# Sharing out the expert gathers of a two-layer encoder: 8 : 8 : 7 over three chunks, and 110 instead of 50 left for the next layer

## The chip, the cores and the metric

The kernel runs on one core of a Trainium2 chip. The metric is the time of one execution on the device in microseconds (us). A run is timed several times; the figure of a kernel is the median.

## What is computed

The reference runs two layers over 512 tokens of width 1024, one sequence. Each layer is an attention stage and an expert stage:

```python
for l in range(DEPTH):                                    # 2
    sh1, sc1, g1, sh2, sc2, g2 = split(silu(c) @ ada_w[l] + ada_b[l], 6)
    h = modulate(x, sh1, sc1)                             # layer norm, scale, shift
    mix = hybrid_mixer(h, ...)                            # three kinds of heads, one w_in, one w_o
    x = layer_norm(ALPHA * x + (1 + g1) * mix, ln1_g[l], ln1_b[l])
    h = modulate(x, sh2, sc2)
    # peer: per token and head, the 16 best of 128 * 128 experts
    q = (h @ wq).reshape(S, 8, 2, 128)
    v1, i1 = top_k(q[..., 0, :] . sub_k1, 16); v2, i2 = top_k(q[..., 1, :] . sub_k2, 16)
    experts, g = best 16 of the 16 * 16 sums v1 + v2, softmax of them
    act = gelu(u_tab[experts] . h)                        # u_tab, v_tab: 16384 rows of 1024 f32
    ffn = sum over the 8 * 16 experts of (g * act) * v_tab[experts]
    x = layer_norm(ALPHA * x + (1 + g2) * ffn, ln2_g[l], ln2_b[l])
```

## The kernel before

The 512 tokens are four blocks of 128. The attention stage of a layer handles blocks 0 and 1 first and then 2 and 3: `prepare` normalises a block's rows of x (`xs0` to `xs3`; tile `ytok`, line 253), `project` multiplies by w_in (two blocks share each weight tile; its first vector step on a block is `kr`, L407), `attend` does the heads (`mx` L506, `sm` L513, `pr` L515), `output` multiplies by w_o, `between` does the two normalisations around the residual sum, `queries` multiplies by the query weights and takes the 16 best keys (`tk_v`, L617), and `topk` (L624) picks the experts: 16 pairs of `tk_hot` (VectorE, L665), `tk_pick` (GpSimd) and `tk_ef` (VectorE, L668), then `eidx` (L669).

The expert sums are done in two ways. Blocks 1 and 2 (`DENSE`) run through **all** experts: `dense` goes over 128 rows of 128 experts each. It loads the row's part of both tables (`u`, `v`, 512 KB each, issued by SyncE), transposes u on TensorE (`utp`, L817), splits it into a rounded half and the rest (`uh` ScalarE L819, `ul` VectorE L821), multiplies (`sp`, L831 to L833), applies the gelu and the gate tile G (`ge`, L837) and accumulates (`acc`, L849). G is built in three chunks of 43, 42 and 43 expert rows (`CUTS`): the first chunk before row 0, the second while the rows of the first are done, the third while those of the second are done (`build`: `o` on VectorE, `pg` on TensorE, L804). In the rows of the third chunk nothing is built.

Blocks 0 and 3 are **gathered**: `experts` fetches, for each of the 128 slots of a token, one row of `u` and one of `v` per partition with an indirect DMA from GpSimd's queue (512 KB, tile `g`, four buffers, L696 and L708), and VectorE reduces each in one instruction (a dot product L698, or a weighted sum L713). This text calls such an instruction a gather sum. A layer has 2 blocks x 2 tables x 128 = 512 of them. When all sums of a block are done, `finish` writes the block's new rows of x (`xs0`, `xs3`), which the next layer's `prepare` reads.

`experts` is a generator, and `pace(ex, mark, n)` takes n steps from it. The calls to `pace` share the 512 gathers of a layer out: `EARLY[l]` ahead of the dense part, one beside each of the 32 builds of the first chunk, `LATE[l]` at the start of the next layer's attention stage (L903), and the rest beside the 128 expert rows (L955). A scheduler then orders each engine's instructions; what is written earlier has the higher priority. Each engine takes its instructions strictly in that order.

Of the kernel before, what the change touches and what calls it, by code (L numbers as in the profile page):

```python
# [30 lines left out]
PH, NK, TOPK = 8, 128, 16  # L31
TG = 8
TI = 2
CUTS = (0, 43, 85, 128)
DENSE = (1, 2)
EARLY = (80, 110)
LATE = (50, 0)
WK = 4
ADK = 2
HB = 2  # L40
# [13 lines left out]
def body(ctx, tc, x, c, positions, ada_w, ada_b, w_in, q_norm_g, kv_norm_g, w_uq, w_ukv, conv_w,  # L54
# [16 lines left out]
    def open_attention(l):  # L71
        A.stack = ExitStack()
        A.fix = A.stack.enter_context(tc.tile_pool(name=f"afix{l}", bufs=1))
        A.w = A.stack.enter_context(tc.tile_pool(name=f"aw{l}", bufs=1))
        A.bufs = BUFS[l]
        A.work = A.stack.enter_context(tc.tile_pool(name=f"awork{l}", bufs=1))
        A.small = A.stack.enter_context(tc.tile_pool(name=f"asmall{l}", bufs=2))
        A.ps = A.stack.enter_context(tc.tile_pool(name=f"aps{l}", bufs=1, space=PSUM))
        if l == 0:
            A.ad = A.stack.enter_context(tc.tile_pool(name="ad", bufs=1))  # L80
# [208 lines left out]
    def layer_setup(l):  # L289
        y = Layer()  # L290
        y.l = l
        y.hT = {}
        y.sc1 = A.fix.tile([P, KT], F32, name="sc1")
        nc.sync.dma_start(y.sc1, mod[l, D:2 * D].rearrange("(k p) -> p k", p=P))
        y.sh1 = A.fix.tile([P, KT], F32, name="sh1")
        nc.sync.dma_start(y.sh1, mod[l, 0:D].rearrange("(k p) -> p k", p=P))
        y.qg = A.fix.tile([P, 2], F32, name="qg")
        nc.sync.dma_start(y.qg, q_norm_g[l].rearrange("(k p) -> p k", p=P))
        y.kvg = A.fix.tile([P, 1], F32, name="kvg")
        nc.sync.dma_start(y.kvg, kv_norm_g[l].rearrange("(k p) -> p k", p=P))  # L300
        y.cw = A.fix.tile([P, 2, 3], F32, name="cw")
        for ci in range(2):
            nc.sync.dma_start(y.cw[:, ci, :], conv_w[l, :, ci * P:(ci + 1) * P].rearrange("w p -> p w"))
        y.sqT = A.fix.tile([P, 2, HS, P], F32, name="sqT")
        nc.vector.memset(y.sqT, 0.0)
        y.kT = A.fix.tile([QH + NB, HM, S], F32, name="kT")
        maskk = block_rows(64, P, NEG)
        nc.scalar.copy(y.kT[QH:QH + NB].rearrange("p h (b k) -> p h b k", b=NB),
                              maskk[QH:QH + NB, None, :, :].to_broadcast([NB, HM, NB, P]))
        y.v = A.fix.tile([P, NB, HM * VD], F32, name="v")  # L310
        y.skT = A.fix.tile([P, 2, S], F32, name="skT")
        y.sv = A.fix.tile([P, NB, HS * DS], F32, name="sv")
        y.uT = A.fix.tile([P, 2, P + 2], F32, name="uT")
        nc.vector.memset(y.uT[:, :, 0:2], 0.0)
        return y

    def layer_rows(y):
        l = y.l
        y.rows = rows[l]
        rf = A.work.tile([96, 256], F32, name="rf", tag="q", bufs=2)  # L320
        r = 0
        for src in (ln1_g[l:l + 1, :], ln1_b[l:l + 1, :], mod[l:l + 1, 4 * D:5 * D], mod[l:l + 1, 3 * D:4 * D],
                    mod[l:l + 1, 5 * D:6 * D], ln2_g[l:l + 1, :], ln2_b[l:l + 1, :],
                    mod[l:l + 1, 2 * D:3 * D]):
            nc.sync.dma_start(rf[r:r + 4, :], src.rearrange("o (c n) -> (o c) n", n=256))
            r += 4
        for p in range(3):
            if p:
                nc.sync.dma_start(rf[32 * p:32 * p + r, :], rf[0:r, :])
            q = slice(32 * p, 32 * p + 32)  # L330
            for k in range(p + 1):
                nc.vector.tensor_copy(rows[l][q], rf[q])
                if k < p:
                    nc.vector.tensor_tensor(rf[q], rf[q], rows[l][q], op=OP.subtract)

    def layer_keys(y):
        l = y.l
        y.keysT = A.fix.tile([P, 2 * PH, NK], F32, name="keysT")
        for i, src in enumerate((peer_k1, peer_k2)):
            kst = A.w.tile([P, PH, P], F32, name="kst", tag="w", bufs=A.bufs["w"])  # L340
            nc.sync.dma_start(kst, src[l].rearrange("h n d -> n h d"))
            for h0 in range(0, PH, 4):
                pt = A.ps.tile([P, 4, P], F32, name="pt", tag="tr", bufs=2)
                for j in range(4):
                    nc.tensor.transpose(pt[:, j, :], kst[:, h0 + j, :], ident)
                nc.scalar.copy(y.keysT[:, 2 * h0 + i:2 * (h0 + 4) + i - 1:2, :], pt)
# [11 lines left out]
    def prepare(y, b):  # L358
        hT = A.work.tile([P, KT, P], F32, name="hT", bufs=2)
        yt = A.work.tile([P, D], F32, name="ytok", bufs=1)  # L360
        normalize(yt, xs[b])
        transpose_cols(hT, yt, KT, scale=y.sc1, bias=y.sh1)
        y.hT[b] = hT
# [210 lines left out]
    def between(y, b, rt, mk=None):  # L574
        l = y.l
        row_op(y, rt, rt, 7, OP.mult, mk)
        nc.vector.scalar_tensor_tensor(rt, xs[b], ALPHA, rt, op0=OP.mult, op1=OP.add)
        affine(y, xs[b], rt, rt, 0, 1, mk)
        h2 = A.work.tile([P, D], F32, name="h2d", tag="tok", bufs=2)
        affine(y, h2, h2, xs[b], 2, 3, mk)  # L580
        h2T = A.work.tile([P, KT, P], F32, name="h2T", tag="tok", bufs=2)
        transpose_cols(h2T, h2, KT, tag="tr" if mk else "mm")
        if b in DENSE:
            slot = DENSE.index(b) * P
            nc.sync.dma_start(h2scr[l][:, :, slot:slot + P], h2T)
        else:
            nc.sync.dma_start(h2tok[l][b // 2], h2)
        v1 = topp.tile([P, 2 * PH, TOPK], F32, name="tk_v", bufs=2)
        fi = topp.tile([P, PH, 2, TOPK], F32, name="tk_f", bufs=2)
        return h2T, v1, fi  # L590
# [303 lines left out]
    def pace(ex, mark, n):  # L894
        gate[0] = mark
        for _ in range(n):
            next(ex)

    ada_first(range(4))
    for l in range(L):  # L900
        if l:
            open_attention(l)
            late()  # L903
        y = layer_setup(l)

        def pick(b, v1, fi):
            return topk(l, v1, fi, b, b not in DENSE)

        res = [None] * NB
        for b in (0, 1):  # L910
            prepare(y, b)
        layer_keys(y)
        ps = project(y, (0, 1))
        if l + 1 < L:
            ada_side(0, range(4, 12))
        layer_rows(y)
        behind = None
        for p in ps:
            b = p[0]
            attend(y, *p)  # L920
            if b == 1:
                for b2 in (2, 3):
                    prepare(y, b2)
            h = between(y, b, output(y, b, p[2]))
            r = queries(y, *h, range(4))
            if b == 0:
                behind = r
            res[b] = pick(b, *h[1:])
        p2, p3 = project(y, (2, 3), behind)
        if l + 1 < L:  # L930
            ada_side(1, range(12))
        attend(y, *p2)
        h = between(y, 2, output(y, 2, p2[2]))
        queries(y, *h, range(2))
        attend(y, *p3)
        rt = output(y, 3, p3[2])
        queries(y, *h, range(2, 4))
        res[2] = pick(2, *h[1:])
        h = between(y, 3, rt, lambda: A.ps.tile([P, 512], F32, name="prow", tag="at", bufs=2))
        queries(y, *h, range(4))  # L940
        res[3] = partial(pick, 3, *h[1:])
        A.stack.close()
        dn = dense(y, DENSE, res)
        ex = chain.from_iterable(experts(y, b, *res[b]) for b in range(NB) if b not in DENSE)
        pace(ex, None, EARLY[l])
        groups = 2 * P // TG
        for _ in range(groups):
            mark = next(dn)
            pace(ex, mark, 1)
        with tc.issue_after(mark.ins):  # L950
            res[3] = res[3]()
        n = 2 * 2 * NSLOT - EARLY[l] - LATE[l] - groups
        for a, mark in enumerate(dn):
            if a < NK:
                pace(ex, mark, (a + 1) * n // NK - a * n // NK)  # L955
        late = partial(pace, ex, mark, LATE[l])
        if not l + 1 < L:
            late()
# [22 lines left out]
```

## Time and profile before

| | us |
|---|---|
| median of three runs | 3564.16 |
| lowest, highest | 3544.61, 3568.53 |
| profiled execution, its span | 3550.53, 3548.8 |

The profile is one execution, so its stretches add up to its own span, some 14 us under the median. Over the whole span TensorE is busy 87%, VectorE 78%, GpSimd 42% and ScalarE 26%. [...]

### The profile page before, as it was taken

What the parts mean: (1) busy time and instruction counts of PE and PEld (TensorE: products, weight loads), DVE (VectorE), ACT (ScalarE), POOL (GpSimd) and SP (SyncE); (2) the same over time, 40 slices, a digit from 0 to 9 for tenths busy, and PEclk for the clock granted to TensorE, in tenths of its full rate; (3) what the DMA queues carried; (4) which work ended last, traced back from release to release, by engine and by line L of the source; (5) the groups of instructions that cost most, each with busy time, mean ns of one, the idle gap of its engine ahead of it and who ended that gap; (6) DMA issues with size and microseconds to landing.
All of it is one profiled execution on the core that took longest, in us unless ns stands there. A gap on an engine that the chain in (4) does not pass through costs nothing.

```text
span 3548.8 us, 54489 instructions
## 1 busy us (share of the span) xinstructions
PE 3072.0 (87%) x19708; PEld 2258.0 (64%) x19708; DVE 2765.7 (78%) x6277; ACT 927.4 (26%) x1860; POOL 1476.2 (42%) x1347
## 2 busy tenths in 40 slices
PE   7889768658999999999948896776699999999998
PEld 4657536536777776777736774555467767777775
DVE  4668996999777877776675579889998778776777
ACT  2342432222222222222222223312222222222221
POOL 1025573256343334444462045534454434444543
PEclk9989889859999999999979996997699999999998
DMA  9777978568898888899986586885789988989997
GB/s 276 221 230 251 313 261 287 174 187 282 306 322 307 316 310 310 311 348 344 337 288 206 173 292 211 296 294 178 238 275 350 333 312 316 331 323 335 358 353 256
DMA packets 430173, 1012.14 MB, mean 285 GB/s; under 512 B 40504, under 2 KB 229192, under 8 KB 429904
## 3 DMA queue, kind: packets, MB, share of 16 engines
q0 software_dynamic: 147456, 536.94, 42.5%
q1 hardware_dynamic: 282448, 471.73, 39.6%
q8 instruction: 156, 2.56, 0.3%
q14 instruction: 113, 0.93, 0.1%
HBM read 1002.06 MB, written 6.34 MB: 284 GB/s over the span
## 4 chain that ended last, share of the span: by engine, by line
PE 13%; DVE 13%; DMA 10%; issue 9%; POOL 4%; ACT 1%; SPq 0%; POOLq 0%; DVEq 0%; ACTq 0%
DMA g<-in_peer_v,eidx 5%; PE pm L157 4%; PE acc L849 3%; DVE acc L713 2%; POOL g L696 2%; DVE g L698 2%; DMA g<-in_peer_u,eidx 2%; DVE tk_ef L668 1%; PE sp L831 1%; PE sp L832 1%; PE sp L833 1%; PE utp L817 1%; DMA wt<-in_peer_wq 1%; POOL g L708 1%; DVE o L797 1%
## 5 line engine op out<-in xcount | busy, mean ns | idle before, releaser
L708 POOL DMA_INDIRECT g<-in_peer_v,eidx x512 | 613.4, 1198 | 782.0 <-DVE acc L713 481.7
L849 PE MATMUL acc<-v,ge 128*128 128x512 f32 x2048 | 928.9, 595 | 6.4 <-DVE ge L837 5.8
L696 POOL DMA_INDIRECT g<-in_peer_u,eidx x512 | 603.2, 1178 | 764.4 <-DVE g L698 499.9
L713 DVE SCALAR_TENSOR_TENSOR acc<-g,wts,acc 128x1024 f32<-128x1024 f32 x508 | 674.2, 1327 | 145.1 <-DMA g<-in_peer_v,eidx 137.7
L698 DVE SCALAR_TENSOR_TENSOR g<-g,h 128x1024 f32<-128x1024 f32 x512 | 620.3, 1225 | 172.9 <-DMA g<-in_peer_u,eidx 161.8
L831 PE MATMUL sp<-hh,uh 128*128 128x256 f32 x2048 | 613.7, 300 | 1.6 <-ACT ge L835 0.9
L849 PEld LDWEIGHTS acc<-v,ge 128*128 128x128 f32 x2048 | 370.3, 190 | 370.7 <-issue 364.1
L833 PE MATMUL sp<-hh,ul 128*128 128x256 f32 x2048 | 594.8, 290 | 0.0
L832 PE MATMUL sp<-hl,uh 128*128 128x256 f32 x2048 | 583.7, 285 | 0.0
L819 ACT CAST uh<-utp 128x512 fp32r<-128x512 f32 x512 | 304.1, 595 | 871.9 <-PE utp L817 710.9
L821 DVE TENSOR_TENSOR ul<-utp,uh 128x512 fp32r<-128x512 f32 x512 | 347.6, 684 | 110.5 <-ACT uh L819 104.2
L831 PEld LDWEIGHTS sp<-hh,uh 128*128 128x128 f32 x2048 | 392.4, 192 | 7.6 <-issue 5.5
L832 PEld LDWEIGHTS sp<-hl,uh 128*128 128x128 f32 x2048 | 392.1, 191 | 5.3 <-issue 5.3
L833 PEld LDWEIGHTS sp<-hh,ul 128*128 128x128 f32 x2048 | 391.4, 191 | 0.1
L817 PE MATMUL utp<-ident,u 128*128 128x128 f32 x2048 | 302.9, 277 | 49.0 <-DVE ul L821 46.5
L817 PEld LDWEIGHTS utp<-ident,u 128*128 128x128 f32 x2048 | 236.4, 142 | 126.9 <-issue 70.7
L806 ACT COPY G<-pg 128x344 f32<-128x344 f32 (+1 forms) x192 | 146.8, 765 | 593.9 <-PE pg L804 477.5
L804 PEld LDWEIGHTS <-o 128*128 128x128 bf16 x4608 | 163.3, 102 | 187.4 <-issue 91.9
L804 PE MATMUL pg<-o,o 128*128 128x43 bf16 (+1 forms) x4608 | 183.9, 190 | 104.7 <-DVE o L797 86.4
L157 PE MATMUL pm<-wt,h2T 128*128 128x256 f32 x1024 | 235.9, 385 | 17.6 <-DMA wt<-in_peer_wq 16.7
L157 PE MATMUL pm<-wt,hT 128*128 128x256 f32 (+1 forms) x1024 | 232.4, 380 | 12.6 <-ACT hT L274 6.3
L157 PEld LDWEIGHTS pm<-wt,h2T 128*128 128x128 f32 x1024 | 193.3, 193 | 51.0 <-DMA wt<-in_peer_wq 21.5
(235 smaller groups left out, 3448.2 us busy)
## 6 DMA issues: line engine op xcount, KB each, us to landing
u<-in_peer_u SPq DMA_DIRECT2D x256, 512.0 KB
v<-in_peer_v SPq DMA_DIRECT2D x256, 512.0 KB
wt<-in_peer_wq SPq DMA_DIRECT2D x128, 512.0 KB
adw<-in_ada_w SPq DMA_DIRECT2D x160, 256.0 KB
wt<-in_w_o SPq DMA_DIRECT2D x64, 512.0 KB
wt<-in_w_in SPq DMA_DIRECT2D x56, 512.0 KB
wt<-in_ada_w SPq DMA_DIRECT2D x16, 512.0 KB
g<-in_peer_u,eidx POOLq DMA_INDIRECT x512
```

What stands on the lines that cost most here:

```text
L157: r = nc.tensor.matmul(pm[:, c0:c0 + m], lhsT=lhsT[:, k0 + k, :], rhs=wt[:, k, :m], start=k0 + k == 0, stop=k0 + k == KT - 1)
L696: nc.gpsimd.indirect_dma_start(out=g, out_offset=None, in_=u_flat, in_offset=bass.IndirectOffsetOnAxis(ap=eidx[:, h, k:k + 1], axis=0))
L698: after(nc.vector.scalar_tensor_tensor(out=g, in0=g, scalar=1.0, in1=h2, op0=OP.mult, op1=OP.mult, accum_out=dots[:, h, k:k + 1]))
L708: nc.gpsimd.indirect_dma_start(out=g, out_offset=None, in_=v_flat, in_offset=bass.IndirectOffsetOnAxis(ap=eidx[:, h, k:k + 1], axis=0))
L713: r = nc.vector.scalar_tensor_tensor(out=acc, in0=g, scalar=wts[:, h, k:k + 1], in1=acc, op0=OP.mult, op1=OP.add)
L804: nc.tensor.matmul(pg[:, tt, 0:n], lhsT=o2[:, tt // TI, :, tt % TI], rhs=o1a[:, tt // TI, p, 0:n, tt % TI], start=tt == 0 and p == 0, stop ...
L817: nc.tensor.transpose(pt[:, j * P:(j + 1) * P], u[:, k * P:(k + 1) * P], ident)
L821: nc.vector.tensor_tensor(ul.rearrange("p j t -> p (j t)"), pt, uh.rearrange("p j t -> p (j t)").bitcast(F32), op=OP.subtract)
L831: nc.tensor.matmul(sp, lhsT=uh[:, j, :], rhs=hh[:, k, :], start=k == 0, stop=False)
L832: nc.tensor.matmul(sp, lhsT=uh[:, j, :], rhs=hl[:, k, :], start=False, stop=False)
L833: nc.tensor.matmul(sp, lhsT=ul[:, j, :], rhs=hh[:, k, :], start=False, stop=k == KT - 1)
L849: nc.tensor.matmul(acc[i][g], lhsT=w[:, i * P:(i + 1) * P], rhs=v[:, g * 512:(g + 1) * 512], start=a == 0, stop=a == NK - 1)
```

## The change

The number of gathers of layer 0 that wait for layer 1's attention stage goes from 50 to 110, and the gathers beside the expert rows are no longer spread evenly: a row of the chunks 0, 1 and 2 has the weight 8, 8 and 7. For layer 0 that leaves 512 - 80 - 110 - 32 = 290 beside the rows instead of 350. For layer 1 it stays at 370, with the new weights.

```diff
 EARLY = (80, 110)
-LATE = (50, 0)
+LATE = (110, 0)
+SHARE = (8, 8, 7)
...
         n = 2 * 2 * NSLOT - EARLY[l] - LATE[l] - groups
+        upto = [0]
+        for s, (c0, c1) in zip(SHARE, zip(CUTS, CUTS[1:])):
+            upto += [upto[c0] + s * (i + 1) for i in range(c1 - c0)]
         for a, mark in enumerate(dn):
             if a < NK:
-                pace(ex, mark, (a + 1) * n // NK - a * n // NK)
+                pace(ex, mark, upto[a + 1] * n // upto[NK] - upto[a] * n // upto[NK])
         late = partial(pace, ex, mark, LATE[l])
```

In the changed program the lines behind L37 are one further on, so that the gather sums are L699 and L714 there. What the scheduler makes of it on VectorE, at three places. The first is the start of the heads of block 0 in layer 1, before; 53 gather sums of layer 0 stand ahead of it, and none are left:

```order
L244 BN_STATS bnst<-acc 128x6 x2
L506 TENSOR_REDUCE mx<-sc 128x4
L246 BN_AGGR bnmv<-bnst 128x2
L232 SCALAR_TENSOR_TENSOR acc<-acc,bnmv,prow 128x512
L506 TENSOR_REDUCE mx<-sc 128x4
L232 SCALAR_TENSOR_TENSOR acc<-acc,bnmv,prow 128x512
L513 RECIPROCAL sm<-sm 128x4
L515 TENSOR_TENSOR pr<-pr,sm 128x512
L232 SCALAR_TENSOR_TENSOR xs_98<-acc,rs_r,prow 128x512 x2
```

The same place after (`xs_98` is `xs3`):

```order
L507 TENSOR_REDUCE mx<-sc 128x4
L699 SCALAR_TENSOR_TENSOR g,dots<-g,h_11911 128x1024
L507 TENSOR_REDUCE mx<-sc 128x4
L699 SCALAR_TENSOR_TENSOR g,dots<-g,h_11911 128x1024
L514 RECIPROCAL sm<-sm 128x4
L516 TENSOR_TENSOR pr<-pr,sm 128x512
L699 SCALAR_TENSOR_TENSOR g,dots<-g,h_11911 128x1024 x3
L514 RECIPROCAL sm<-sm 128x4
L516 TENSOR_TENSOR pr<-pr,sm 128x512
```

Again 53 gather sums stand ahead, and from there to `eidx` of block 0 another 60 stand between the attention's own steps. The finish of block 3 has gone from here. Second, where it now stands: among the last steps of `topk` of block 0, after.

```order
L233 SCALAR_TENSOR_TENSOR xs_98<-acc,rs_r,prow 128x512
L666 TENSOR_TENSOR tk_hot<-iotaj,tk_tib 128x400
L669 TENSOR_REDUCE tk_ef<-tk_pick 128x8
L247 BN_AGGR bnmv<-bnst 128x2 x2
L233 SCALAR_TENSOR_TENSOR rt<-rt,bnmv,prow 128x512 x2
L254 TENSOR_SCALAR ytok<-xs_98,bnmv,rs_r 128x1024
L233 SCALAR_TENSOR_TENSOR xs_96<-rt,rs_r,prow 128x512 x2
L670 CAST eidx_17995<-tk_ef 128x128
```

Before, that `ytok` of block 3 stood ahead of the first `tk_v` of block 0, one `ytok` behind the other:

```order
L253 TENSOR_SCALAR ytok<-xs_97,bnmv,rs_r 128x1024
L232 SCALAR_TENSOR_TENSOR h2d<-h2d,rs_r,prow 128x512 x2
L246 BN_AGGR bnmv<-bnst 128x2
L555 SCALAR_TENSOR_TENSOR sbe<-ntri,z 128x512
L253 TENSOR_SCALAR ytok<-xs_98,bnmv,rs_r 128x1024
L546 SCALAR_TENSOR_TENSOR sp_18247<-z,sbe 128x512
L617 MAX tk_v<-scs 128x8 x4
```

It moved behind the 60 gather sums and nearly all of `topk`. Third, expert row 22 of layer 0, in the first chunk, before:

```order
L837 TENSOR_TENSOR ge<-ge,G 128x256
L713 SCALAR_TENSOR_TENSOR acc<-g,wts,acc 128x1024 x2
L788 TENSOR_TENSOR o_8676<-iotab,i2T 128x1024
L792 TENSOR_TENSOR o_8678<-iotab,i1T 128x4x84
L713 SCALAR_TENSOR_TENSOR acc<-g,wts,acc 128x1024
L821 TENSOR_TENSOR ul<-utp,uh 128x512
L797 TENSOR_TENSOR o_8678<-o_8678,gT 128x4x84 x3
```

And after:

```order
L838 TENSOR_TENSOR ge<-ge,G 128x256
L714 SCALAR_TENSOR_TENSOR acc<-g,wts,acc 128x1024
L789 TENSOR_TENSOR o_8649<-iotab,i2T 128x1024
L793 TENSOR_TENSOR o_8651<-iotab,i1T 128x4x84
L798 TENSOR_TENSOR o_8651<-o_8651,gT 128x4x84 x2
L822 TENSOR_TENSOR ul<-utp,uh 128x512
L798 TENSOR_TENSOR o_8651<-o_8651,gT 128x4x84
```

The row has lost two of its three gather sums ahead of `ul`; other rows lose none. Counted in VectorE's order from each `ge` of the first row of a chunk to that of the next (the last: to row 127), layer 0 goes from 117, 115 and 115 gather sums to 103, 98 and 86; layer 1 from 124, 120 and 120 to 128, 128 and 111. From the last row of layer 0 to the first of layer 1 there are 196 before and 255 after. Ahead of row 0 of layer 0 there are 112 in both, and behind the last row of layer 1 five before and three after.

## Rows read from the trace of the kernel before

**Rows 1.** Busy time by stage: columns PE, PEld, DVE, ACT, POOL, then clock, DMA.

```profile
781.00:1135.00 354.00, 329.65 (x2427) 241.86 (x2428) 290.65 (x574) 87.86 (x163) 159.21 (x133) 0.98 0.86 301
1135.00:1472.00 337.00, 327.92 (x2462) 242.40 (x2461) 261.13 (x460) 84.75 (x159) 133.86 (x117) 0.99 0.87 311
1472.00:1772.60 300.60, 300.60 (x1677) 218.31 (x1676) 210.40 (x293) 64.70 (x126) 137.85 (x115) 1.00 0.92 340
1772.60:1910.00 137.40, 87.34 (x387) 66.50 (x385) 95.06 (x165) 33.99 (x78) 72.91 (x68) 0.81 0.90 295
1910.00:2075.00 165.00, 145.19 (x757) 117.62 (x758) 96.16 (x347) 47.89 (x123) 27.63 (x42) 0.94 0.50 150
2075.00:2300.00 225.00, 174.07 (x757) 123.30 (x757) 195.76 (x505) 69.45 (x144) 108.80 (x106) 0.83 0.83 279
2300.00:2532.80 232.80, 153.34 (x1343) 119.86 (x1341) 210.34 (x689) 57.01 (x91) 96.08 (x77) 0.78 0.70 230
2532.80:2883.00 350.20, 332.76 (x2420) 242.39 (x2421) 301.36 (x581) 86.64 (x162) 158.42 (x142) 0.98 0.88 314
2883.00:3216.30 333.30, 321.40 (x2436) 237.77 (x2436) 260.64 (x456) 83.82 (x159) 135.69 (x121) 0.99 0.90 324
3216.30:3516.70 300.40, 300.40 (x1676) 218.11 (x1675) 214.01 (x308) 64.12 (x127) 138.35 (x119) 1.00 0.94 348
```

**Rows 2.** The same stretches, GpSimd's gather issues alone (x is their count).

```profile
781.00:1135.00 354.00, 142.68 (x117) 0.98 0.86 301
1135.00:1472.00 337.00, 133.07 (x115) 0.99 0.87 311
1472.00:1772.60 300.60, 137.85 (x115) 1.00 0.92 340
1772.60:1910.00 137.40, 62.66 (x49) 0.81 0.90 295
1910.00:2075.00 165.00, 3.91 (x4) 0.94 0.50 150
2075.00:2300.00 225.00, 92.21 (x86) 0.83 0.83 279
...
2532.80:2883.00 350.20, 137.53 (x124) 0.98 0.88 314
2883.00:3216.30 333.30, 135.69 (x121) 0.99 0.90 324
```

**Rows 3.** Waits of TensorE in the rows of layer 0's first chunk, 781 to 1135.

```profile
PE utp L817 <- DVE ul L821: 17.4, 12, 2.8
PE pg L804 <- DVE ul L821: 5.6, 4, 2.7
```

**Rows 4.** Costliest groups of the page: the weighted gather sum.

```profile
L713 DVE SCALAR_TENSOR_TENSOR acc<-g,wts,acc 128x1024 f32<-128x1024 f32 x508 | 674.2, 1327 | 145.1 <-DMA g<-in_peer_v,eidx 137.7
```

**Rows 5.** Costliest VectorE group of 2075 to 2300: the dot product of a gather.

```profile
L698 DVE SCALAR_TENSOR_TENSOR g<-g,h 128x1024 f32<-128x1024 f32 x54 | 65.5, 1215 | 17.5 <-DMA g<-in_peer_u,eidx 13.0 <-issue 4.3
```

**Rows 6.** Waits of VectorE from 1910 to 2075, the longest three.

```profile
DVE tk_v L617 <- ACT scs L608: 31.0, 4, 11.8
DVE rt L230 <- PE prow L227: 8.8, 1, 8.8
DVE sp L546 <- ACT sbe L544: 8.0, 2, 5.5
```

**Rows 7.** Chain of waits, 1890 to 1912: the last gather of layer 0.

```profile
1904.15 5.94 DMA g<-in_peer_v,eidx
```

**Rows 8.** Timeline of VectorE in layer 1: ytok of block 3, eidx of block 0, first mx of block 2.

```profile
1972.51 0.81 DVE L253 TENSOR_SCALAR ytok<-xs,bnmv,rs_r 128x1024 f32<-128x1024 f32 x1 [1.07 <-PE pt L265]
...
2068.87 0.23 DVE L669 CAST eidx<-tk_ef 128x128 int32<-128x128 f32 x1
...
2145.18 0.54 DVE L506 TENSOR_REDUCE mx<-sc 128x1 f32<-128x384 f32 x1
```

## The prediction

> **What bounds the kernel now.** I read the stages first, as busy time by stretch, then in each stretch the waits of the engine that sets its pace. The rows of layer 0's third chunk are bound by TensorE and nothing else: it is busy 300.60 of 300.60 us at a clock of 1.00 [rows 1], which is 7.16 us for each of the 42 steps from its first row to its last. 115 gathers run beside them and delay nothing [rows 2]. Layer 1's third chunk reads the same, 300.40 of 300.40 us. In the first two chunks TensorE is busy 329.65 of 354.00 and 327.92 of 337.00 us [rows 1]: it stands idle for 24.4 and 9.1 us, above all because `ul` comes late from VectorE, 17.4 and 5.6 us in the first chunk [rows 3]. VectorE has 82% and 77% of these stretches filled and takes its work in order, so a gather sum that waits for its data holds up the `ul` behind it.
>
> Layer 1's attention stage, from the last row of layer 0 at 1772.6 to the first row of layer 1 at 2532.8, is another thing. From 1772.6 to 1910 the DMA engines are busy 0.90 of the time; the weights and the late gathers share them. From 1910 to 2075 no gather sum is left until `eidx` of block 0 is known: TensorE is busy 145.19 of 165 us, VectorE only 96.16, and the DMA share is 0.50 [rows 1]; four gathers are issued there, at its end [rows 2]. This is the place where the change puts its 60. From 2075 on VectorE is the bound: 195.76 of 225.00 us and 210.34 of 232.80 us, 87% and 90% [rows 1].
>
> **What the change takes away.** Layer 0's rows lose 14, 17 and 29 gather sums in the three chunks. A dot product takes 1.215 us [rows 5] and a weighted sum 1.327 us [rows 4], so VectorE is spared about 18, 22 and 37 us. The 29 of the third chunk are worth nothing, since TensorE has no idle time there to give back: the cover is TensorE itself, and it stays. What the other 31 can bring is at most the idle time of TensorE, 24.4 + 9.1 = 33 us, and at least nothing. Where in between? Layer 1 gives a second sample: its first chunk has 124 gathers issued against 117, and yet TensorE idles less there, 350.20 - 332.76 = 17.4 us; its second has 121 against 115 and idles 333.30 - 321.40 = 11.9 us [rows 1, 2]. Seven more gathers go with seven us less in one chunk, six more with three us more in the other, so the idle time depends on where a gather stands at least as much as on how many there are. I take 10 us of the 33.
>
> **What it adds in layer 1's rows.** 4 and 8 more gather sums in the first two chunks, 9 fewer in the third. The nine bring nothing for the reason above. The twelve are 15 us of VectorE against 29 us of idle TensorE; I take +2 us, between 0 and +8 (half of them in the open).
>
> **What it adds in the attention stage.** 60 gather sums come between the first `mx` of block 0 and `eidx` of block 0: the last 28 dot products and 32 weighted sums of layer 0, 28 x 1.215 + 32 x 1.327 = 76 us of VectorE. The stretch from 1910 to 2075 has 165 - 96 = 69 us of idle VectorE. Its work comes to 96 + 76 = 172 us, so even with no idle time left the stretch is 7 us longer than now. That is the lower bound. How well can VectorE be filled where gathers and attention steps mix? Two rows tell: 87% from 2075 to 2300, with 86 gathers issued, and 95.06 of 137.40, 69%, from 1772.6 to 1910, with 49 [rows 1, 2]. At 87% the stretch takes 172 / 0.87 = 198 us, 33 more; at 69% it takes 249, 84 more. I take the first: at 198 us the DMA engines would move 150 x 165 + 60 x 524 KB = 56 MB at 285 GB/s, which is what the stretch from 2075 moves (279 GB/s at a share of 0.83), while the poorer one had its DMA at 0.90. The longest idle pieces of VectorE now, 31.0 us for `scs`, 8.8 for `prow` and 8.0 for `sbe` [rows 6], are waits for TensorE and ScalarE that a gather sum can fill. What cannot vanish is the wait for a gather's data: the last one now lands 5.94 us after its issue [rows 7], and with four buffers GpSimd's next issue waits for a sum. The small steps of the normalisations on GpSimd (`ve`, `rs_r`) queue behind such an issue, and VectorE waits for them. SyncE's weight loads stand apart, on another queue.
>
> Is the delay given back later? Behind `eidx` of block 0 VectorE has the same work as before to the first row (143 and 142 gather sums) and is 87% to 90% busy already. So I let the 33 us through in full.
>
> [...]
>
> **The sum.** +33 - 10 + 2 = +25 us on the profiled execution of 3550.5, so 3575.5. The median of the three runs lies 13.7 higher, and I place the forecast halfway, at 3557.3 + 25 = **3582 us**. Its own ends: the stage between +7 and +84 with most weight near +33, the rows between -33 and 0.
>
> **The rivals.**
>
> First, slower: block 3 becomes what the stage waits for. Its `ytok` now stands at 1972.51, 96 us ahead of `eidx` of block 0, and the first `mx` of block 2 follows `eidx` by 76 us, `ytok` by 172.7 us [rows 8]. After the change the order puts `ytok` of block 3 some 8 us ahead of `eidx`. Both blocks of `project` share their weight tiles, so block 2 cannot be finished without it. VectorE's order has 41 gather sums between `eidx` and that `mx` instead of 25, which moves `mx` by some 16 x 1.3 = 20 us, plus the top-16 steps of block 1, to about 116 us behind `eidx`. If the chain from `ytok` to `mx` takes less than 124 us, VectorE does not notice. If it takes the 172.7 us of now, VectorE stands still for about 49. For it: the profile shows 172.7. Against it: in the present order `project` also waits for the queries of block 0, which will be done by then. I price it at +35 on top of the forecast: 3617 us.
>
> Second, the gathers hide: VectorE's idle time and the half-idle DMA engines take the 60 nearly whole, +7, and three quarters of TensorE's idle time in the two chunks go, -25, +2: 3541 us. For it speaks the DMA share of 0.50, against it that the order of VectorE is fixed and 172 us of work must fit without a hole.
>
> Third, TensorE's clock. In the stretch from 1772.6 to 1910, where TensorE is busy 87 of 137 us, the granted clock is 0.81, and from 1910, busy 145 of 165, it is 0.94 [rows 1]. If gather sums ahead of `mx`, `pr` and `rt` starve it so that the clock falls to 0.81 there too, its 145.2 us become 145.2 x 0.94 / 0.81 = 168, +23 on the forecast: 3605 us. [...]
>
> That the change does not do what it says is ruled out by the order: the 60 sums have moved.
>
> **How the numbers follow.** Chances: forecast 0.50, block 3 late 0.25, hidden 0.17, clock 0.08. Within 1% is what a measurement of this kernel cannot tell from no change; that is 3528.5 to 3599.8 around the median. The rival with block 3 lies above it unless its stall is small (0.22 of 0.25), the clock mostly (0.05), and the forecast with a worse filled stage in 0.06: slower 0.33. Faster by over 1% would take all 33 us of the rows and a free stage, 3557.3 - 33 + 7 = 3531, and even that falls short; I leave 0.05 for the scatter of the runs, 3544.61 to 3568.53. The same: 0.62. The range leaves out the better half of the hidden case (0.08) and the worst of the first rival and of the stage (0.11): 3541 to 3625.
>
> **What would show it.** In the profile after: the third chunk of layer 0 still 300.6 us with TensorE never idle; the first two chunks together 691 us now, and some 10 fewer; layer 1's rows within a few us of 350, 333 and 300; from the first `mx` of block 0 to `eidx` of block 0 some 33 us more, with VectorE near 87%; from that `eidx` to the first row of layer 1 the same 464 us as now. If that last stretch grows, with VectorE idle ahead of the first `mx` of block 2, it is the first rival; if `eidx` comes on time, the second. The forecast is wrong if the rows of the third chunk get shorter, or if the time behind `eidx` shrinks and gives the delay back.

## The result: 0.8% slower, by terms that were not those of the sum

The changed kernel takes 3586.45 us (median of 8 runs, 3578.78 to 3591.31) against 3564.07 us (8 runs): a ratio of 1.0077, 95% interval 1.006 to 1.0093. The forecast was 3582. Its sum came out, two of its three terms did not. The profiled execution has a span of 3583.9 us, 35.1 more than before.

Busy time by stage after the change, the expert rows alone: the three chunks of layer 0, then those of layer 1 (columns as in [rows 1]; the edges are the starts of `ge` of rows 0, 43, 85 and 127).

```profile
781.00:1130.70 349.70, 332.84 (x2442) 244.00 (x2443) 273.43 (x550) 87.60 (x163) 138.00 (x119) 0.98 0.80 282
1130.70:1465.30 334.60, 324.27 (x2446) 240.40 (x2446) 241.11 (x428) 83.90 (x160) 118.60 (x100) 0.99 0.81 288
1465.30:1766.10 300.80, 300.80 (x1677) 218.30 (x1677) 176.81 (x258) 64.53 (x125) 114.55 (x86) 1.00 0.78 291
...
2594.40:2934.10 339.70, 327.98 (x2414) 239.67 (x2415) 308.67 (x598) 86.91 (x162) 157.98 (x146) 0.99 0.90 326
2934.10:3254.10 320.00, 320.00 (x2447) 236.92 (x2446) 270.11 (x471) 84.46 (x160) 137.90 (x129) 1.00 0.96 351
3254.10:3554.60 300.50, 300.50 (x1677) 218.23 (x1676) 206.18 (x289) 64.66 (x126) 133.85 (x110) 1.00 0.91 336
```

Layer 0's chunks take 349.7, 334.6 and 300.8 us against 354.0, 337.0 and 300.6 [rows 1]: 6.5 less in all between the first row and the last. In the third chunk TensorE is busy throughout, as before, and the 29 gathers fewer brought nothing. But layer 1's chunks take 339.7, 320.0 and 300.5 us against 350.2, 333.3 and 300.4, **24 less**, although the first two carry 128 and 129 gathers instead of 124 and 121. In the second of them TensorE is busy 320.00 of 320.00 us; before it was 321.40 of 333.30 [rows 1].

What VectorE waited for in that second chunk, first before (waits, total us, times, longest), then what TensorE waited for:

```profile
DVE g L698 <- DMA g<-in_peer_u,eidx: 24.1, 20, 3.5
DVE acc L713 <- DMA g<-in_peer_v,eidx: 22.2, 17, 2.7
```

```profile
PE utp L817 <- DVE ul L821: 9.4, 7, 2.6
```

And after, in the same chunk, where TensorE waits for nothing:

```profile
DVE g L699 <- DMA g<-in_peer_u,eidx: 12.3, 19, 1.2
...
DVE acc L714 <- DMA g<-in_peer_v,eidx: 8.8, 9, 3.0
```

The waits of VectorE for a gather's data have fallen from 46.3 us to 21.1, and the 9.4 us that TensorE waited for `ul` behind them are gone.

The attention stage, from the last row of layer 0 to the first `mx`, to `eidx` of block 0, to the first `mx` of block 2, to the first row of layer 1. Before:

```profile
1772.60:1919.20 146.60, 93.97 (x410) 71.14 (x409) 101.13 (x178) 36.54 (x84) 72.91 (x68) 0.80 0.86 281
1919.20:2068.90 149.70, 132.59 (x704) 107.86 (x702) 88.23 (x331) 42.12 (x107) 23.71 (x38) 0.96 0.50 151
2068.90:2145.20 76.30, 70.41 (x352) 56.78 (x351) 58.42 (x225) 24.00 (x57) 28.17 (x28) 1.00 0.98 348
2145.20:2532.80 387.60, 262.96 (x1778) 191.51 (x1778) 349.53 (x972) 105.69 (x188) 180.62 (x159) 0.77 0.72 235
```

After:

```profile
1766.10:1911.80 145.70, 91.54 (x410) 68.08 (x409) 97.95 (x174) 36.41 (x84) 71.95 (x71) 0.81 0.84 284
1911.80:2105.50 193.70, 125.45 (x582) 93.58 (x581) 160.95 (x420) 44.97 (x104) 88.61 (x94) 0.80 0.73 252
2105.50:2238.10 132.60, 107.36 (x476) 84.09 (x474) 100.34 (x360) 29.44 (x68) 54.30 (x53) 0.85 0.87 298
2238.10:2594.40 356.30, 246.56 (x1774) 182.55 (x1774) 304.43 (x833) 110.42 (x190) 153.04 (x135) 0.80 0.71 232
```

It takes 828.3 us instead of 760.2, **68 more**, not 33. From the first `mx` to `eidx` it is 193.7 against 149.7 (+44), with VectorE at 83%; the forecast had 87%. From `eidx` to the first `mx` of block 2 it is 132.6 against 76.3 (+56), and 31 us of that come back behind it. Much of this +56 is work that changed its place: VectorE is busy 42 us more in that piece and 45 us less behind it. From `eidx` to the first row as a whole its work is as before, 405 against 408 us, and the time is 489 against 464: **25 us more**, all of it idle VectorE. VectorE is only 76% busy in the first of the two pieces and waits there, 17.2 us for the data of gathers:

```profile
DVE g L699 <- DMA g<-in_peer_u,eidx: 17.2, 10, 6.3
```

The three steps of [rows 8], on the timeline after:

```profile
2096.71 0.80 DVE L254 TENSOR_SCALAR ytok<-xs,bnmv,rs_r 128x1024 f32<-128x1024 f32 x1
...
2105.51 0.23 DVE L670 CAST eidx<-tk_ef 128x128 int32<-128x128 f32 x1
...
2238.05 0.54 DVE L507 TENSOR_REDUCE mx<-sc 128x1 f32<-128x384 f32 x1
```

`ytok` of block 3 now stands 8.8 us ahead of `eidx` of block 0, where the order had it, and the first `mx` of block 2 follows it by 141.3 us. That is above the 124 us at which the first rival said that VectorE would start to stand still.

### The profile page after: what moved, and what is told of

Its sections match the earlier page's. It is cut to its first block, busy times and chain, and to the rows that moved or that the text cites. A ratio compares the mean times of both kernels' runs of the same rounds, so it can differ in the third digit from the quotient of the medians.

```text
span 3583.9 us, 54456 instructions
## 1 busy us (share of the span) xinstructions
PE 3076.9 (86%) x19708; PEld 2257.7 (63%) x19708; DVE 2770.8 (77%) x6277; ACT 940.9 (26%) x1870; POOL 1473.9 (41%) x1347
## 4 chain that ended last, share of the span: by engine, by line
PE 40%; DVE 23%; DMA 17%; issue 14%; POOL 5%; ACT 1%; SPq 1%; POOLq 0%; DVEq 0%; ACTq 0%
PE acc L850 15%; PE pm L158 6%; DMA g<-in_peer_v,eidx 5%; PE sp L834 4%; PE sp L833 4%; PE sp L832 4%; PE utp L818 4%; DVE g L699 4%; DMA g<-in_peer_u,eidx 3%; DVE acc L714 3%; DMA adw<-in_ada_w 2%; DMA wt<-in_peer_wq 2%; DVE tk_ef L669 2%; POOL g L697 2%; DVE o L798 2%
## 5 line engine op out<-in xcount | busy, mean ns | idle before, releaser
L709 POOL DMA_INDIRECT g<-in_peer_v,eidx x512 | 625.3, 1221 | 839.7 <-DVE acc L714 510.6
L697 POOL DMA_INDIRECT g<-in_peer_u,eidx x512 | 591.3, 1155 | 821.5 <-DVE g L699 542.4
L714 DVE SCALAR_TENSOR_TENSOR acc<-g,wts,acc 128x1024 f32<-128x1024 f32 x508 | 673.2, 1325 | 106.8 <-DMA g<-in_peer_v,eidx 103.2
L699 DVE SCALAR_TENSOR_TENSOR g<-g,h 128x1024 f32<-128x1024 f32 x512 | 622.9, 1231 | 153.1 <-DMA g<-in_peer_u,eidx 152.1
```

The lines of the kernel that those rows point to most:

```text
L697: nc.gpsimd.indirect_dma_start(out=g, out_offset=None, in_=u_flat, in_offset=bass.IndirectOffsetOnAxis(ap=eidx[:, h, k:k + 1], axis=0))
L699: after(nc.vector.scalar_tensor_tensor(out=g, in0=g, scalar=1.0, in1=h2, op0=OP.mult, op1=OP.mult, accum_out=dots[:, h, k:k + 1]))
L709: nc.gpsimd.indirect_dma_start(out=g, out_offset=None, in_=v_flat, in_offset=bass.IndirectOffsetOnAxis(ap=eidx[:, h, k:k + 1], axis=0))
L714: r = nc.vector.scalar_tensor_tensor(out=acc, in0=g, scalar=wts[:, h, k:k + 1], in1=acc, op0=OP.mult, op1=OP.add)
```

## The experiments

Each kernel's ratio is to the kernel before on the same chip, with its 95% interval; stretches are those of its profiled execution, between the same steps as above. Before, the stage is 760 us, layer 0's first two chunks are 354 and 337, layer 1's 350 and 333. One execution has some scatter. Layer 0's second chunk is 334.6, 331.8, 332.1 and 332.2 us in the changed kernel and in three kernels made from it (stale3, thin_dve and no_dma, below), which share its order there; the stage is 760, 757 and 752 us in the kernel before, share_only and even_both, whose order there is nearly the same. The profiled executions of share_only, late_only and thin_dve lie 12, 9 and 17 us under their medians, that of even_early100 lies 8 above.

**The two halves.** The weights alone, and the late gathers alone (the edits are cut to the number that changes):

```diff
-LATE = (110, 0)
+LATE = (50, 0)          # share_only
```
```diff
-SHARE = (8, 8, 7)
+SHARE = (1, 1, 1)       # late_only
```

> LATE back at 50, the weights 8 : 8 : 7 kept. Theory: the 24 us that layer 1's rows lost come from the order of the gather sums, three in nearly every row of the chunks with builds, and the 68 us of the attention stage come from the 60 late gathers alone. Then layer 1's first two chunks stay at about 660 us against 683.5 before, the attention stage is back at 760, layer 0's rows are within 5 us of before (the order there is still uneven): a span of about 3525 us, 24 under before. Rival: the number of gathers in a chunk sets its idle time; then layer 1's rows are only as fast as 128 and 128 gather sums allow, no faster than before, and the span is 3549 or a few us more.

> Even weights, LATE at 110. Theory: layer 1's rows are as before the change (984 us), the attention stage has the whole +68, layer 0's rows lose 5 to 10 us: a span of about 3608 us, some 59 over before. Rival: the late gathers also free layer 1's rows (block 3 settled at another time); then the rows are fast here too, and the span is about 3584, that of the changed kernel.

The weights alone are **faster** than before: 3531.39 us, ratio 0.9942 (0.9921 to 0.9962). Stages of that kernel (chunks 0 and 1 of layer 0, the attention stage, chunks 0 and 1 of layer 1):

```profile
777.10:1126.70 349.60, 330.21 (x2427) 242.19 (x2428) 295.47 (x578) 88.02 (x163) 161.76 (x138) 0.98 0.87 312
1126.70:1470.60 343.90, 328.35 (x2460) 242.65 (x2460) 265.58 (x474) 85.07 (x160) 136.44 (x122) 0.99 0.87 313
...
1771.30:2528.10 756.80, 550.22 (x3238) 420.84 (x3236) 593.68 (x1693) 207.56 (x434) 296.61 (x292) 0.84 0.73 239
2528.10:2867.00 338.90, 326.74 (x2413) 238.79 (x2414) 310.93 (x599) 87.10 (x162) 157.28 (x147) 0.99 0.91 327
2867.00:3188.20 321.20, 321.20 (x2448) 237.38 (x2447) 268.44 (x469) 85.46 (x160) 141.69 (x128) 1.00 0.96 350
```

The late gathers alone are slower: 3617.62 us, 1.0187 (1.0153 to 1.022).

```profile
779.70:1125.90 346.20, 329.14 (x2446) 240.27 (x2447) 272.18 (x545) 87.75 (x163) 138.95 (x117) 0.99 0.82 282
1125.90:1449.10 323.20, 319.60 (x2442) 236.50 (x2441) 233.18 (x423) 84.28 (x159) 112.27 (x94) 1.00 0.83 287
...
1749.90:2585.50 835.60, 575.78 (x3241) 432.35 (x3240) 667.86 (x1792) 219.76 (x444) 367.10 (x353) 0.79 0.76 254
2585.50:2939.20 353.70, 332.97 (x2421) 242.60 (x2421) 301.99 (x582) 86.38 (x162) 160.32 (x142) 0.98 0.88 311
2939.20:3273.20 334.00, 322.48 (x2435) 238.13 (x2434) 260.30 (x457) 84.47 (x159) 139.19 (x120) 0.99 0.90 323
```

So the two parts pull in opposite ways, and each is a theory's: the weights give layer 1's rows their 24 us (338.9 and 321.2) and leave the stage at 757; the late gathers give the stage 836 us and leave layer 1's rows at 354 and 334. The rival that the late gathers also free layer 1's rows has fallen. Two sizes are off. With the weights alone, layer 0's second chunk is 7 us **longer** than before, 343.9, and with the late gathers alone layer 0's two chunks lose 22 us, three times what they lost in the changed kernel. The count at the end of the next part bears on both.

**Number or order.** The changed order of VectorE offers a reason. In layer 1 the new weights come to 370 x 8 / 981 = 3.02 gathers a row in the first two chunks, before it was 2.89. Before, many neighbouring rows of its second chunk have 0, 5, 3 and 4 gather sums; after, nearly every row has three. `pace` ties a sum to the row it was taken beside, so at less than three a row the scheduler, which has room for about three, runs out of them and leaves a row empty. That is read from the order; whether it matters on the chip needs runs. The first gives layer 0 the even order too, by weights of its own for each layer:

```diff
-LATE = (110, 0)
-SHARE = (8, 8, 7)
+LATE = (50, 0)
+SHARE = ((31, 31, 20), (8, 8, 7))
...
-        for s, (c0, c1) in zip(SHARE, zip(CUTS, CUTS[1:])):
+        for s, (c0, c1) in zip(SHARE[l], zip(CUTS, CUTS[1:])):
```

> LATE at 50 and weights of 31 : 31 : 20 in layer 0, 8 : 8 : 7 in layer 1; the order then has three gather sums in nearly every row of the first two chunks of layer 0 as well (131 and 130 in all, against 117 and 115 before). Theory of the even order: layer 0's first two chunks lose 15 to 28 of their 33 us of idle TensorE although they carry 29 more gather sums, and the span is about 3504 us. Rival of the number: 29 more sums of 1.25 us on VectorE cost these chunks 5 to 15 us, and the span is 3530 or more.

3488.6 us, 0.9822 (0.9786 to 0.9858). The three chunks of layer 0 and the stage:

```profile
781.00:1124.10 343.10, 328.33 (x2429) 240.46 (x2430) 305.19 (x586) 87.14 (x163) 165.63 (x146) 0.98 0.91 328
1124.10:1446.30 322.20, 322.20 (x2459) 238.30 (x2458) 276.86 (x483) 84.61 (x160) 147.83 (x133) 1.00 0.96 349
1446.30:1746.80 300.50, 300.50 (x1677) 218.25 (x1676) 176.77 (x256) 64.35 (x125) 111.81 (x87) 1.00 0.79 296
1746.80:2499.00 752.20, 558.97 (x3237) 429.29 (x3235) 595.05 (x1694) 207.71 (x434) 299.56 (x292) 0.83 0.73 241
```

With 131 and 130 gather sums instead of 117 and 115, the two chunks lose 26 us, and in the second TensorE is never idle. More gather sums in even order are faster than fewer in uneven order; the rival of the number has fallen. The span, 3487.6 us, is 16 under the 3504 expected; half of that is the stage, 8 us shorter than before. The second run keeps these totals and makes the order uneven again, by handing the gathers out in pairs of rows:

```diff
-            upto += [upto[c0] + s * (i + 1) for i in range(c1 - c0)]
+            upto += [upto[c0] + s * (i + 1 if c1 == NK or i + 1 == c1 - c0 else (i + 1) // 2 * 2)
+                     for i in range(c1 - c0)]
```

> As even_both, but the gathers of the first two chunks are handed out in pairs of rows, none for one and twice as many for the next. In layer 0 and in the first half of layer 1's second chunk the scheduler still puts three gather sums into nearly every row; in layer 1's first chunk and from row 59 on the order is uneven (0, 5, 3, 4 and the like), with the same totals as in even_both (126 and 127 against 129 and 127). Theory of the even order: layer 0's chunks stay at 343 and 322 us, layer 1's rise from 338 and 321 to 344 to 350 and 325 to 332. If the totals set the time, layer 1's chunks stay within 3 us of 338 and 321.

3510.06 us (two runs), 0.9866 (0.9803 to 0.9929), 18.8 us more span than even_both. Only 12 us of that lie in layer 1's rows. The attention stage is 766.5 us against 752.2, 14 more, with three more gather sums in it; that was not expected and stays open. Layer 0's chunks are 339.9 and 322.5 us, as expected. Layer 1's second is 331.1 against 320.9, as expected; its first is 340.1 against 338.2, where 344 to 350 was expected: the shorter uneven stretch there cost next to nothing. The sharpest view is inside that second chunk, rows 43 to 58 in even order and 58 to 85 in uneven order:

```profile
2845.80:2957.40 111.60, 111.60 (x857) 83.04 (x856) 96.60 (x165) 29.55 (x57) 48.18 (x46) 1.00 0.97 355
2957.40:3177.00 219.60, 210.53 (x1587) 155.35 (x1586) 172.23 (x307) 54.77 (x103) 93.14 (x82) 0.99 0.90 325
```

15 rows in 111.6 us are 7.44 a row, with TensorE never idle; 27 rows in 219.6 us are 8.13 a row, with TensorE idle for 9 us. The gathers issued per row are 3.07 and 3.04. The same two groups of rows in even_both, both in even order:

```profile
2837.20:2952.00 114.80, 114.80 (x867) 84.75 (x866) 97.40 (x166) 29.93 (x57) 51.02 (x46) 1.00 0.96 350
2952.00:3158.10 206.10, 206.10 (x1583) 152.59 (x1582) 172.26 (x307) 54.14 (x103) 89.53 (x83) 1.00 0.96 349
```

Rows 58 to 85 take 206.1 us there, 7.63 a row, with 83 gathers issued instead of 82. So at the same rows and the same number the uneven order costs 13.5 us, 9 of them idle TensorE.

The orders of all these kernels, counted from one `ge` to the next, also tell which part of the unevenness goes with the time. Add up what the rows of a second chunk have **beyond three** gather sums each. It is 5 or 6 in the twelve even ones, which take 319 to 322.5 us. It is 10 in layer 0 of late_only, 323.2 us, although eight of its 42 rows are empty. It is 17 in layer 1 of lumpy2 and in layer 0 of the changed kernel, stale3, thin_dve and no_dma: 331 to 335 us, with 127 gather sums in the one and 98 in the others. It is 25 to 27 in the kernel before (both layers), layer 1 of late_only and layer 0 of share_only: 333 to 344 us. So the two sizes that were off fit the order as well, and it is the overfilled rows that go with the time, not the empty ones. This is a count over the runs there are; no run changed it alone, and among the first chunks lumpy2's in layer 1 is an exception (17, and only 340.1 us).

**What the attention stage pays for.** Three kernels start from the changed one and each leave out one thing. The first lets nothing in layer 1 wait for block 3:

```diff
-        r = affine(y, xs[b], acc, acc, 5, 6, mk, pool)
+        r = affine(y, acc if (y.l, b) == (0, 3) else xs[b], acc, acc, 5, 6, mk, pool)
```

> The changed kernel, except that layer 0 does not write block 3's new rows of x (its last normalisation goes into a spare tile), so that layer 1 reads block 3's rows as they were ahead of the expert stage. All 110 late gathers and their sums stay, but nothing in layer 1 waits for them; ytok of block 3 moves from 113 gather sums behind the last expert row to 83, next to that of block 2. If part of the +68 us of the stage is block 3 being late, the stage falls from 828 us to 790 to 805, with the piece from eidx of block 0 to the first mx of block 2 back near 80 from 132. If it is the work of the 60 sums alone, it stays at 820 or above.

3553.02 us, 1.0005 (0.9985 to 1.0026). The stage is 792.6 us, inside the range for a late block 3; its last three pieces:

```profile
1912.40:2108.00 195.60, 158.99 (x781) 126.17 (x779) 165.08 (x428) 52.89 (x126) 92.89 (x95) 0.89 0.83 281
2108.00:2168.50 60.50, 55.75 (x271) 44.62 (x270) 47.24 (x183) 17.68 (x40) 23.43 (x23) 0.97 0.98 339
2168.50:2558.90 390.40, 265.14 (x1784) 193.56 (x1783) 353.85 (x1001) 106.31 (x190) 181.48 (x164) 0.74 0.74 244
```

From the first `mx` to `eidx` next to nothing has changed (195.6 against 193.7), so the work of the 60 sums costs there what it did. But from `eidx` to the first `mx` of block 2 it is 60.5 us instead of 132.6, with 34 of that lost again behind it. The piece alone misleads, since the order changed with it (20 gather sums in it instead of 41). Behind `eidx` as a whole it is 450.9 us here, 488.9 in the changed kernel and 463.9 before, with 401, 405 and 408 us of VectorE's work. So 36 us of the stage go when nothing waits for block 3 at all (26 us of the time, by the ratios 1.0077 and 1.0005). Against the kernel before, the stretch behind `eidx` had grown by only 25; whether that kernel pays the other 13 for block 3 too was not run. Of the 68 us, then, **25 to 36 are block 3 being late**, and 32 to 44 are the sums themselves. The other two take away VectorE's part and the DMA engines' part of the sums:

```diff
+                m = 64 if (y.l, b, h0) == (0, 3, PH - HB) and j >= 4 else D
-                after(nc.vector.scalar_tensor_tensor(out=g, in0=g, scalar=1.0, in1=h2, ...
+                after(nc.vector.scalar_tensor_tensor(out=g[:, :m], in0=g[:, :m], scalar=1.0, in1=h2[:, :m], ...
```
```diff
+                own = (y.l, b, h0) == (0, 3, PH - HB) and j >= 4
+                if not own:
                     nc.gpsimd.indirect_dma_start(out=g, ...
-                after(nc.vector.scalar_tensor_tensor(out=g, in0=g, ...
+                after(nc.vector.scalar_tensor_tensor(out=g, in0=h2 if own else g, ...
```

The weighted sums of these gathers are cut in the same way.

> The changed kernel with the last 60 gather sums of layer 0 taken over 64 of the 1024 columns, so those experts' part of block 3 is left out; the gathers themselves stay. VectorE is spared some 67 us at the place where the 60 stand. If VectorE's time is the cost, the stage falls from 828 to 760 to 780 us. If the pace of the gathers or the lateness of block 3 is, it stays at 800 or above.

3582.17 us, 1.0091 (1.007 to 1.0113); the stage is 813.8 us, inside the second range, so VectorE's time is not the whole cost.

```profile
1907.30:2062.10 154.80, 106.21 (x538) 81.48 (x536) 93.70 (x395) 39.64 (x93) 74.20 (x85) 0.87 0.88 313
2062.10:2216.00 153.90, 112.08 (x519) 89.09 (x519) 120.14 (x386) 32.78 (x78) 72.08 (x70) 0.84 0.89 303
2216.00:2575.30 359.30, 250.56 (x1776) 185.55 (x1774) 299.43 (x833) 112.32 (x192) 143.48 (x127) 0.78 0.66 211
```

The first piece is 154.8 us, 5 more than in the kernel before, with all 60 gathers still issued: VectorE's time is what the 60 sums cost **there**. But the scheduler then put `ytok` of block 3 behind `eidx`, 26 us later, and the second piece is 153.9 us, the longest of all. TensorE is busy 112 of 154 us in it, and 16 us of its waits there are for block 3's last steps (`acc`, `xs`, `ytok`); the order also has 55 gather sums in this piece instead of 41. The run separates the two costs only within their pieces, not in the total.

> The changed kernel with the last 60 gathers of layer 0 left out; their 60 sums stay at full width and read the h2 tile instead, so the result of block 3 lacks those experts. The DMA engines are spared 31 MB and no sum of these waits for a landing. If VectorE's time is the cost, the stage stays at 800 to 820 us. If waiting for the gathers is, it falls to 760 to 780.

3551.67 us, 0.9996 (0.9972 to 1.0019); the stage is 793.3 us, between the two ranges.

```profile
1919.10:2099.90 180.80, 138.20 (x685) 111.29 (x686) 151.73 (x409) 52.81 (x116) 26.11 (x38) 0.83 0.40 123
2099.90:2176.50 76.60, 71.62 (x363) 58.22 (x361) 58.67 (x224) 24.13 (x57) 30.04 (x28) 1.00 1.00 353
2176.50:2558.20 381.70, 260.16 (x1774) 191.33 (x1774) 348.04 (x963) 104.97 (x187) 174.87 (x158) 0.75 0.73 238
```

The first piece gets 13 us shorter than in the changed kernel (its order has nine of the 60 sums ahead of the first `mx`) and stays 31 above before, with VectorE at 84% and the DMA engines at 0.40: the sums' own time again. The second is back at 76.6, and block 3 is done 55 us earlier (`ytok` 63.6 us ahead of `eidx` instead of 8.8). That is the order's doing: 113 gather sums stand ahead of this `ytok` in both kernels, but 210 instructions of VectorE stand between it and `eidx` here and 15 in the changed kernel. So the run shows once more that the second piece is short where block 3 comes early. What waiting for landings costs it does not show, as the order changed with it.

**Versions that go further.** If 60 more late gathers cost 68 us, 30 fewer than before may give some back:

```diff
-LATE = (50, 0)
-SHARE = ((31, 31, 20), (8, 8, 7))
+LATE = (20, 0)
+SHARE = ((31, 31, 27), (8, 8, 7))
```

> As even_both, but 20 instead of 50 late gathers; the third chunk of layer 0 takes the 30 (31 : 31 : 27, 116 gather sums, as many as it hid before). If each late gather costs the attention stage what the 60 of the change did, 68 / 60 = 1.1 us, the stage loses 34 us: a span of about 3470 us. Rival: the first 50 late gathers lie beside waits for weights and for block 3's neighbours and cost little; then the stage loses under 10 us, and the span is 3495 to 3504.

3471.07 us, 0.9784 (0.9748 to 0.9821). Third chunk of layer 0 and the stage:

```profile
1445.90:1745.80 299.90, 299.90 (x1675) 218.57 (x1674) 209.18 (x307) 63.09 (x126) 125.81 (x116) 1.00 0.95 346
1745.80:2479.60 733.80, 549.11 (x3240) 423.59 (x3238) 560.24 (x1642) 207.42 (x434) 270.25 (x262) 0.84 0.69 226
```

The stage loses 18.4 us against even_both, and the medians differ by 17.5: 0.6 a gather, half the price that the 60 had, and more than the rival's. Of the 18.4, 16 lie between the last row and the first `mx`. That the span, 3467.6 us, meets the 3470 expected is luck: even_both was already 16 under its own figure. The third chunk takes 116 gathers for nothing, at 299.90 of 299.90 us busy. The last run moves ten early gathers of layer 1 as well:

```diff
-EARLY = (80, 110)
-SHARE = ((31, 31, 27), (8, 8, 7))
+EARLY = (80, 100)
+SHARE = ((31, 31, 27), (31, 31, 27))
```

> As even_late20, with 100 instead of 110 early gathers in layer 1 and weights of 31 : 31 : 27 there too, so that the ten go beside the expert rows (130, 130 and 117 gather sums, three in nearly every row of the first two chunks). Layer 1's attention stage is bound by VectorE (87 to 90% busy before), so ten sums fewer should shorten it by 10 to 13 us, and the third chunk hid 120 sums before: a span of about 3457 us. If the stage has slack there, or if the rows do not take the ten for nothing, the span stays at 3467.

3471.21 us, 0.9762 (0.9741 to 0.9784): by the median no different from even_late20, though the two intervals leave room for a few us. The profiled execution is the longest of four. The stage and layer 1's first chunk in it:

```profile
1748.20:2483.70 735.50, 551.05 (x3239) 424.69 (x3237) 548.70 (x1621) 207.86 (x433) 265.16 (x252) 0.84 0.67 218
2483.70:2827.10 343.40, 331.96 (x2416) 243.06 (x2417) 309.53 (x597) 89.19 (x162) 157.79 (x148) 0.98 0.91 327
```

The stage shows no gain from the ten (735.5 against 733.8 us), and the first chunk is 343.4 us against 339.1. In this execution layer 0's first chunk, whose order is the same in both kernels, is 3 us longer too, so differences of that size say little. The 10 to 13 us expected are not in the median, so this expectation was wrong. Whether something other than VectorE's sum of work sets the stage there stays open.

## Why the prediction came out, term by term

**Third chunks bound by TensorE: right.** About 300 us in every kernel whatever they carried: 86 gathers in layer 0 of the changed kernel, 116 in even_late20.

**Layer 0's rows, -10 us: right in size**, -6.5, but not for the reason of fewer sums. late_only has about as few and lost 22, and even_both has 29 more and lost 26.

**Layer 1's rows, "I take +2 us": the step that failed**, measured at -24. It priced twelve more gather sums by their work on VectorE against idle TensorE. The text had just seen that idle time depended "on where a gather stands at least as much as on how many there are", and then counted how many. Where they stand could be read beforehand: the order of layer 1 went from 0, 5, 3, 4 to 3, 3, 3, 3. share_only shows the effect with the rest undone, and lumpy2 shows it at the same rows of one chunk.

**The attention stage, +33: half of it.** Where the forecast put the cost, between the first `mx` and `eidx`, it is +44: the share of 87% was taken from another stretch, and VectorE came to 83%. The assumption that failed is that nothing more happens behind `eidx`. The same 464 us were expected there, and it took 489, with as much work on VectorE as before. The first rival happened **as well**: block 3 late, priced at 35, worth 25 against the kernel before and 36 against stale3. Forecast and rival were taken as alternatives, and they come one after the other. Their prices add up to the measured +68, but neither price was exact.

**The clock rival** did not decide. Between the first `mx` and `eidx` the granted clock (its mean in the piece, as a share of full speed) did fall, from 0.96 to 0.80, as TensorE went from 133 of 150 us busy to 125 of 194. But in stale3 the clock there is 0.89 and the piece is as long as in the changed kernel, and in thin_dve it is 0.87 and the piece is 41 us shorter than in stale3. So the clock is not what makes the piece long.

**The hidden case** fell: the stage grew by 68, and VectorE waited 14.2 us for landings ahead of `eidx` and 17.2 behind it. The profile after has medians of 6.9 and 6.8 us from issue to landing for the gathers of `u` and `v`, against the 5.94 us of the one in [rows 7].

The sum, -10 + 2 + 33 = +25, met a span of +35 and a median of +22. That it came so near is luck: layer 1's rows came out 26 us below their term and the attention stage 35 above its own, and the two errors nearly cancel. The total alone would have hidden both.

## What to carry to other kernels

Where one engine takes its work in order and serves two streams, look at how evenly the side work stands between the steps of the main one, and not only at its sum: here 3.02 a row were 24 us faster in layer 1 than 2.89, with hardly a row overfilled. When work is pushed into a later stage, ask not only what idle time it fills but which result it delays, and add the two prices where they come one after the other. A change whose parts pull apart is worth splitting: one half of this one is 0.6% faster than before, and followed up it is 2.2% faster.

## What was not expected of the hardware

In even order the second chunks run TensorE without any idle time at a DMA share of 0.96 and 349 to 351 GB/s, more than the 0.87 to 0.90 and 311 to 325 GB/s of the uneven ones that carry about as many gathers (before, share_only's layer 0, late_only's layer 1, the uneven rows of lumpy2). So the DMA engines had room. In layer 1's second chunk GpSimd's gather issues waited 179.8 us for gather sums before, up to 9.2 us at a time, and 152.4 us after, up to 3.2. That four gather buffers, given back in bursts, kept the DMA engines from using their room is argued from the order and these waits and was not tried with more buffers.
